# First layer's down projection as seven products, with the next mixer's input split beside its last steps

## The chip, the cores and the metric

The kernel runs on one core of one Trainium2 chip. The metric is the device time of one execution in microseconds (us), taken as the median of several runs; before the change it is 2800.11 us (three runs, 2799.79 to 2801.98).

## The reference, cut to what matters

One inference step of a two-layer encoder trunk on 1024 prompt frames and 32 sample frames (T = 1056 columns here), model width 1024:

```python
for i in range(DEPTH):                       # layer 0: retention, layer 1: GLA
    h = rmsnorm(x, norm_mix[i])
    x = x + mixer(h)
    h = rmsnorm(x, norm_ffn[i])
    u = h @ w_up                             # 1024 -> 2 * 2816
    c = causal_conv3(u) + conv_b
    gate, val = split(c)
    x = x + (silu(gate) * val) @ w_down      # 2816 -> 1024
y = rmsnorm(x, norm_final)
```

The change is about the last product of layer 0, `(silu(gate) * val) @ w_down`, and about the norm and first projections of layer 1's mixer (GLA) behind it. Everything is float32; each operand of a product is split into a rounded high part and a low remainder, and a product is three matmuls on TensorE: high by high, high by low, low by high.

## The kernel before, in words

**Layout.** The width lies on the partitions in tiles of 128, time lies along the free dimension. `XA`, `XB` and `XH` are large tiles that hold split operands; `AR` and `HR` hold float32 intermediates. `scr_x` in HBM holds the residual stream x. `R` holds the norm's factor for each column, the same on all partitions.

**Up projection** (`seven`, L331 to L441; `ffn_up`, L1905 on). It runs in both layers by seven products in place of eight: operands are cut into 2 by 2 quarters, sums of quarters are formed on VectorE, and a bank of 264 columns is accumulated for each of seven products (matmuls of lines 436, 440 and 441). After each of the 22 feature tiles `conv` makes the hidden tile. In layer 1 `pair_sums` (L1953 on) then forms the sums that seven products need and writes them to `scr_h7`; in layer 0 `conv` writes the plain hidden tile to `scr_h`.

**Down projection, layer 0** (`Down`, L1417 on). Three chunks of 384, 384 and 288 columns (`CM`); in each, 22 hidden tiles times 8 output tiles times 3 matmuls, lines 1519 to 1521. When a chunk is done, `evict` (L2221 on) adds the product to x (L2223), splits x for the mixer (`split_x`: ACT cast at L162, VectorE remainder at L163), squares it (`sumsq`, L147, and adds at L158 on VectorE and GpSimd in turn) and stores it. The norm of chunks 0 and 1 (`rms_a`, `rms_b`: L181 to L207) is made within the next chunk's steps, that of chunk 2 as a "tail" in the mixer's first steps. `rms_a` reduces the sum of squares over the partitions by matmuls against ones (L189), takes the root on ACT and VectorE (L174 to L179), and spreads it into a diagonal (`dg`, L199); `rms_b` multiplies the diagonal by ones (L205) and copies the result to `R` (L207).

**Down projection, layer 1** (`Down7`, L1602 on). Hidden tiles go in 11 pairs, output tiles in 4 pairs, and 14 windows n = 0 to 13 slide over the pairs: the widths are 1, 2, 3, eight times 4, 3, 2, 1 pairs. The windows of three and four take seven products, the others eight plain ones ("plain"), each over two column halves s, lines 1702 to 1704, 264 columns each. Up to window 9 the results are added to `scr_x` by accumulating DMAs on GpSimd's queue (L1769); from window 10 on they are added on VectorE to a fetched copy of x (`settle`, L1776 on, and L1719), squared (`squares`, L1796 on) and, behind the final norm (`row`, `root`, `out`), written as y. Weights come raw on SyncE's queue (L1649, L1654) and are split by ACT and VectorE (L1664, L1665; sums at L1684 to L1691).

**The mixer** (`gla`, L1050 on). Its first steps, in the order in which they are written: the gate's features for chunk 0 (`gates_in`, L1354 on; its result is scaled by `R` at L1361), the q and k products of head 0, chunk 0 (`proj`, L133 to L135), their scaling by `R` (`qk_out`), the gate (ACT and VectorE, with a scan at L1099), the tail norm of chunk 2, the features of chunks 1 and 2, then `weigh` (differences on GpSimd at L1122, exponentials on ACT, products on VectorE at L1128 and L1129) and the scores on TensorE (L1165 on).

**What sets the order.** The code is written step by step; a scheduler then orders each engine's queue by that order and by what it expects to be ready, so neighbouring steps may change places. An engine executes its own queue in order and waits at the first instruction whose inputs are not there. Tiles in a reused place wait for the last use of the old tile.

Of the kernel before, what the change touches and what calls it, by code (L numbers as in the profile page):

```python
# [9 lines left out]
F32 = mybir.dt.float32  # L10
# [6 lines left out]
P = 128  # L17
# [33 lines left out]
def trunk_kernel(ctx: ExitStack, tc: tile.TileContext, io):  # L51
# [129 lines left out]
    def rms_a(ss, c, ps, again=False, after=None):  # L181
        i = uid()
        if again and c == 2:
            for s_ in ss:
                G.tensor_copy(s_[:, 288:384].rearrange("p (j t) -> p j t", j=3),
                              s_[:, 256:288].unsqueeze(1).to_broadcast([P, 3, TS]))
        for m in range(3):
            for s_ in ss:
                mm = PE.matmul(ps[:, m:m + 1], s_[:, m * P:m * P + P], ones[:, 0:1],  # L189
                               start=s_ is ss[0], stop=s_ is ss[-1])  # L190
                if after is not None:
                    order(mm, after)
# [10 lines left out]
    def rms_b(dg, c, ps, copy=True):  # L203
        c0, n = CM[c]
        mm = PE.matmul(ps[:, :n], ones, dg.rearrange("p m t -> p (m t)")[:, :n], start=True, stop=True)  # L205
        if copy:
            S.copy(R[:, c0:c0 + n], ps[:, :n])  # L207
        return mm
# [266 lines left out]
    def gla_constants(gp):  # L475
# [7 lines left out]
        nc.sync.dma_start(ba, io["ba"])  # L483
        nc.sync.dma_start(smask, io["smask"])
        nc.sync.dma_start(dmask, io["dmask"])
        nc.sync.dma_start(lmask, io["lmask"])
# [9 lines left out]
        V.tensor_tensor(w2s[64:96], w2r, w2s[0:32].bitcast(F32), op=ALU.subtract)  # L496

# [552 lines left out]
    def gla(closers):  # L1050
# [303 lines left out]
        def gates_in(c):  # L1354
            c0, n = CM[c]
            ps = pp.tile([P, 512], F32, tag="pj", name=f"pa{c0}", bufs=2)
            for kt in range(KT):
                PE.matmul(ps[:32, :n], wa[:, kt], xh[:, kt, c0:c0 + n], start=kt == 0, stop=False)
                PE.matmul(ps[:32, :n], wa[:, kt], xl[:, kt, c0:c0 + n], start=False, stop=kt == KT - 1)
            ar = g1.tile([32, GH * GDK], F32, tag="asr", name=f"asr{c0}")  # L1360
# [16 lines left out]
        gates_in(1)  # L1377
        gates_in(2)
# [25 lines left out]
    scr_h = io["scr_h"]  # L1404
# [197 lines left out]
    class Down7:  # L1602

        def __init__(self, sm, regions, AR, HR):
            self.sm, self.AR, self.HR = sm, AR, HR
# [8 lines left out]
            homes = [list(range(7)), list(range(8, 15)), list(range(16, 22)) + [15], list(range(22, 28)) + [7]]  # L1614
            self.place = {(k, m): homes[k % 4][i] for k in range(NP) for i, m in enumerate(ORD)}
            self.place.update({(0, 8): 7, (1, 8): 15, (NP - 2, 8): 22, (NP - 1, 8): 23})
# [4 lines left out]
            self.sq = [HR[:, 4 * TH + j * TH:5 * TH + j * TH] for j in range(3)]  # L1621
# [23 lines left out]
        def raw_weights(self, n):  # L1645
            h, o = len(self.win[n]) * P, self.offs[n]
            if self.plain[n]:
                r = raw_tile(f"dr{uid()}")[:, :4 * h]
                nc.sync.dma_start(r, io["w_down7"][o:o + 4 * h * P].rearrange("(p c) -> p c", p=P))  # L1649
                return r  # L1650
            rs = []
            for j in range(2):
                r = raw_tile(f"d{'gv'[j]}{uid()}")[:, :2 * h]
                nc.sync.dma_start(r, io["w_down7"][o + j * 2 * h * P:o + (j + 1) * 2 * h * P].rearrange("(p c) -> p c", p=P))  # L1654
# [140 lines left out]

        def squares(self, p, s, half):  # L1796
            t0, n = 2 * TH * s + TH * half, TH
            y = self.Y[p][:, :, t0:t0 + n]
            ss = self.SS[s][:, TH * half:TH * half + n]
            for j in range(2):  # L1800
# [6 lines left out]
                (V if p == 2 and s and half else G).tensor_tensor(ss, ss, sq, op=ALU.add)  # L1807
# [27 lines left out]
        def early(self, s, i):  # L1835
            x0 = {1: [(0, 0, 2)], 2: [(0, 2, 2)], 3: [(0, 4, 2)], 4: [(0, 6, 2)], 5: [(1, 0, 2)], 6: [(1, 2, 2)]}
            x1 = {4: [(1, 4, 2)], 5: [(1, 6, 2)]}
            for a in (x1 if s else x0).get(i, []):
# [567 lines left out]
```

## Time and profile before

| | us |
|---|---|
| median of three runs | 2800.11 |
| lowest, highest | 2799.79, 2801.98 |
| the profiled execution's own time | 2802.62 |
| its span from first to last instruction | 2800.8 |
| layer 0's down projection in it (1340.44 to 1598.74) | 258.30 |
| layer 1's down projection in it (2544.06 to 2787.64) | 243.58 |

The granted TensorE clock of that execution is 0.997 of full speed. The profile page gives busy time by engine, the span in 40 slices, the chain of work that ended last, and groups of instructions by source line; the views of the trace used below are the table by stretches of time ("windows": length, then busy time and instruction count of each engine, granted clock, share of DMA busy, GB/s), the groups by line and shape (count, busy time, mean ns of one, idle time before), the waits, and the timeline.

### The profile page before, as it was taken

How to read it: one execution, taken by the hardware profiler on the slowest of the kernel's cores; microseconds unless marked ns; L12 is line 12 of the kernel's file. 1: busy time of each engine (PE TensorE's matmuls, PEld its weight loads, DVE VectorE, ACT ScalarE, POOL GpSimd, SP SyncE). 2: the span in 40 equal slices, each digit the busy share in tenths (PEclk: the TensorE clock that was granted, in tenths of full speed). 3: DMA queues.
4: the chain of work that ended last, by engine and by line, in shares of the span. 5: the costliest groups of instructions: out<-in, count | busy, mean ns of one | idle time of the engine just before them, and what ended most of it. 6: DMA issues, size and time to landing. Idle time of an engine off the chain costs nothing.

```text
span 2800.8 us, 54530 instructions
## 1 busy us (share of the span) xinstructions
PE 2758.4 (98%) x21990; PEld 2669.3 (95%) x21990; DVE 1972.2 (70%) x3387; ACT 1357.2 (48%) x2481; POOL 370.9 (13%) x637
## 2 busy tenths in 40 slices
PE   9999999999999999999999999999999999999997
PEld 9999988888999999999999989999999999999997
DVE  6876666676557877777555577775479888888666
ACT  7444354444435444444444466663355444445445
POOL 0000000000112111111000032220132111112113
PEclk9999999999999999999999999999999999999999
DMA  6233455554875222222855501115532433329783
GB/s 239 87 115 104 140 150 148 149 146 117 281 251 183 84 77 85 69 85 76 270 183 171 179 30 53 53 46 200 185 124 95 147 128 108 100 89 300 199 227 106
DMA packets 239006, 390.71 MB, mean 139 GB/s; under 512 B 58848, under 2 KB 163424, under 8 KB 234400
## 3 DMA queue, kind: packets, MB, share of 16 engines
q1 hardware_dynamic: 225712, 339.14, 37.3%
q0 software_dynamic: 12496, 47.54, 6.4%
q8 instruction: 172, 2.82, 0.4%
q14 instruction: 82, 0.67, 0.1%
q10 hardware_dynamic: 544, 0.54, 0.1%
HBM read 270.08 MB, written 117.07 MB: 138 GB/s over the span
## 4 chain that ended last, share of the span: by engine, by line
PE 81%; DVE 8%; ACT 3%; POOL 3%; issue 2%; DMA 2%; SPq 0%; DVEq 0%; ACTq 0%; POOLq 0%
PE pu L441 13%; PE pu L436 13%; PE pu L440 13%; PE pd L1519 6%; PE pd L1521 6%; PE pd L1520 6%; PE psv L270 2%; PE psv L271 2%; PE psv L272 2%; PE pu L1702 2%; POOL x L1122 2%; PE pu L1703 2%; PE pu L1704 2%; PE pg L133 1%; PE pg L134 1%
## 5 line engine op out<-in xcount | busy, mean ns | idle before, releaser
L110 DVE TENSOR_TENSOR wlo<-raw,whi 128x1024 fp32r<-128x1024 f32 x131 | 163.4, 1251 | 127.3 <-ACT whi L110 119.4
L415 ACT COPY HR<-pu 128x264 f32<-128x264 f32 x264 | 98.8, 375 | 278.6 <-PE pu L441 272.6
L110 ACT CAST whi<-raw 128x1024 fp32r<-128x1024 f32 x131 | 136.9, 1049 | 174.3 <-PE pd L1520 109.4
L441 PE MATMUL pu<-XA,wgl 128*128 128x264 f32 x752 | 213.4, 284 | 0.0
L436 PE MATMUL pu<-XA,wgh 128*128 128x264 f32 x752 | 212.8, 283 | 0.1
L440 PE MATMUL pu<-XA,wgh 128*128 128x264 f32 x752 | 212.5, 283 | 0.0
L1942 DVE SCALAR_TENSOR_TENSOR AR<-AR,cw 128x1058 f32<-128x1058 f32 x88 | 115.9, 1319 | 72.0 <-ACT AR L1941 63.7
L1915 DVE TENSOR_TENSOR AR<-HR,pu 128x264 f32<-128x264 f32 (+2 forms) x440 | 144.5, 370 | 4.5 <-PE pu L441 4.4
L1520 PE MATMUL pd<-hl,whi 128*128 128x384 f32 (+1 forms) x440 | 142.1, 323 | 0.1
L1519 PE MATMUL pd<-hh,whi 128*128 128x384 f32 (+1 forms) x440 | 142.1, 323 | 0.0
L1521 PE MATMUL pd<-hh,wlo 128*128 128x384 f32 (+1 forms) x440 | 141.7, 322 | 0.0
L436 PEld LDWEIGHTS pu<-XA,wgh 128*128 128x128 f32 x752 | 141.2, 188 | 0.3 <-ACT wgh L372 0.3
L440 PEld LDWEIGHTS pu<-XA,wgh 128*128 128x128 f32 x752 | 141.2, 188 | 0.0
L441 PEld LDWEIGHTS pu<-XA,wgl 128*128 128x128 f32 x752 | 141.0, 188 | 0.0
L436 PE MATMUL pu<-XA,wsh 128*128 128x264 f32 x464 | 132.5, 286 | 1.5 <-DVE ARi L927 0.4
L441 PE MATMUL pu<-XA,wtl 128*128 128x264 f32 x464 | 131.9, 284 | 0.0
L441 PE MATMUL pu<-XA,wsl 128*128 128x264 f32 x464 | 131.8, 284 | 0.0
L436 PE MATMUL pu<-XA,wth 128*128 128x264 f32 x464 | 131.6, 284 | 0.0
L440 PE MATMUL pu<-XA,wsh 128*128 128x264 f32 x464 | 131.4, 283 | 0.0
L440 PE MATMUL pu<-XA,wth 128*128 128x264 f32 x464 | 131.1, 283 | 0.0
L373 DVE TENSOR_TENSOR wtl<-rv,wth 128x1024 fp32r<-128x1024 f32 x58 | 71.0, 1224 | 79.0 <-ACT wth L372 78.9
L1939 POOL COPY cst<-AR 128x2 f32<-128x2 f32 x88 | 51.6, 586 | 564.9 <-DVE AR L1915 564.9
(643 smaller groups left out, 10616.9 us busy)
## 6 DMA issues: line engine op xcount, KB each, us to landing
raw<-w_down SPq DMA_DIRECT2D x60, 512.0 KB, 3.6
rg<-w_up SPq DMA_DIRECT2D x44, 512.0 KB, 3.6
rv<-w_up SPq DMA_DIRECT2D x44, 512.0 KB, 3.5
scr_h<-AR SPq DMA_DIRECT2D x81, 264.0 KB, 2.6
raw<-w_ro SPq DMA_DIRECT2D x39, 512.0 KB, 5.4
XH<-scr_hr POOLq DMA_DIRECT2D x16, 1056.0 KB, 7.1
scr_x<-AR POOLq DMA_DIRECT2D x60, 264.0 KB, 6.5
scr_h<-AR SPq DMA_DIRECT2D x22, 512.0 KB, 2.6
```

What stands on the lines that cost most here:

```text
L110: ins = S.copy(hi, raw), V.tensor_tensor(lo, raw, hi.bitcast(F32), op=ALU.subtract)
L270: PE.matmul(ps, ah, hi, start=kt == 0, stop=False)
L373: split_end[0] = split_last[0] = V.tensor_tensor(l_, src, h.bitcast(F32), op=ALU.subtract)
L415: ins = S.copy(t, b)
L436: mm = PE.matmul(ps, wh[:, k], x[:, 0, kt], start=m in (1, 2, 4, 5) and kt == 0, stop=False, skip_group_check=True)
L440: PE.matmul(ps, wh[:, k], x[:, 1, kt], start=False, stop=False, skip_group_check=True)
L441: mm = PE.matmul(ps, wl[:, k], x[:, 0, kt], start=False, stop=kt == 3, skip_group_check=True)
L1519: PE.matmul(o, w[0][:, k], h[0][:, :n], start=i == 0, stop=False)
L1520: PE.matmul(o, w[0][:, k], h[1][:, :n], start=False, stop=False)
L1521: self.last_mm = PE.matmul(o, w[1][:, k], h[0][:, :n], start=False, stop=i == nk - 1)
L1915: last_put[0] = V.tensor_tensor(u[:, d:d + n], t[:, o:o + n], b[:, o:o + n], op=op)
L1942: V.scalar_tensor_tensor(cj, uj[:, 1:T + 3], cw[:, nt, 1:2], cj, op0=ALU.mult, op1=ALU.add)
```

## The change

Layer 0 now uses `Down7` as layer 1 does, and `Down` is left for the mixers' output products only. Its parts:

1. `conv` calls `pair_sums` in both layers; `scr_h` and the plain branch go. `w_down7` holds both layers' weights.
2. In layer 0 the last windows run both halves of one window before the next window (`seq`), and the end of layer 0 squares 528 columns at a time into `R` (`new_squares`), splits x for the mixer and stores it to `scr_x` (`new_x`), at the steps that `news` lists. The first two mixer weights are loaded after a step of window 12 (`preload`).
3. The norm leaves the down projection. `rms_a` reads one sum of squares, from `R`, with 3 matmuls for a chunk in place of 12. The mixer begins with the q and k products of chunk 0, and each chunk's norm stands around that chunk's gate features (`features_of`).
4. The mixer's small constants are prepared behind the down projection and not ahead of it, the two weights first, the four masks after them.
5. In both layers: other places for the pairs (`homes`), other order of the first loads (`early`), the splits of the first pairs begin three steps earlier. In layer 1: GpSimd's share of the squares in window 13's second half moves to VectorE, and one output product (`out` of quarter 3, first part of the second half) moves from GpSimd to VectorE.

```diff
-    def rms_a(ss, c, ps, again=False, after=None):
+    def rms_a(c, ps):
         i = uid()
...
+        ss = [R[:, t0:t0 + L] for _, t0, L in minors(c)]
+        if c == 2:
+            ss[2] = nps[0].tile([P, 384], F32, tag="sq", name=f"sr{i}", bufs=sqb[0])[:, :P]
+            G.tensor_copy(ss[2].rearrange("p (j t) -> p j t", j=4),
+                          R[:, TP:T].unsqueeze(1).to_broadcast([P, 4, TS]))
         for m in range(3):
...
+            PE.matmul(ps[:, m:m + 1], ss[m], ones[:, 0:1], start=True, stop=True)
```

```diff
-        def gates_in(c):
+        def features_of(c):
             c0, n = CM[c]
-            ps = pp.tile([P, 512], F32, tag="pj", name=f"pa{c0}", bufs=2)
+            ps = lv("pa")
+            dg = rms_a(c, pp.tile([P, GDV], F32, tag="v", name=f"pn{uid()}", bufs=2))
             for kt in range(KT):
                 PE.matmul(ps[:32, :n], wa[:, kt], xh[:, kt, c0:c0 + n], start=kt == 0, stop=False)
                 PE.matmul(ps[:32, :n], wa[:, kt], xl[:, kt, c0:c0 + n], start=False, stop=kt == KT - 1)
+            rms_b(dg, c, lv("pr"))
...
-        gates_in(0)
         p00 = qk_products(0, 0)
+        features_of(0)
         q00 = qk_out(0, p00)
+        features_of(1)
         b00 = gate(0, 0)
-        run_tails(lv)
+        features_of(2)
         for f in closers:
             f()
         g2 = es.enter_context(pool("g2", side="right"))
         units = [(h, c) for h in range(GH) for c in range(3)]
-        gates_in(1)
-        gates_in(2)
```

```diff
+        def new_squares(self, p, s):
+            t = slice(2 * TH * s, 2 * TH * s + 2 * TH)
+            for j in range(2):
+                y = self.Y[p][:, j, t]
+                if p == 3 and j == 0:
+                    S.activation(R[:, t], y, AF.Square)
+                    continue
+                sq = self.sq[self.nsq % 3]
+                self.nsq += 1
+                S.activation(sq, y, AF.Square)
+                (V if p == 2 else G).tensor_tensor(R[:, t], R[:, t], sq, op=ALU.add)
+
+        def new_x(self, p, s):
+            t0, n = 2 * TH * s, 2 * TH
+            y = self.Y[p][:, :, t0:t0 + n]
+            for j in range(2):
+                split_x(2, y[:, j], 2 * p + j, t0, n)
+            nc.sync.dma_start(scr_x[:, 2 * p:2 * p + 2, t0:t0 + n], y)
...
-                (V if p == 2 and s and half else G).tensor_tensor(ss, ss, sq, op=ALU.add)
+                (V if p == 2 and s else G).tensor_tensor(ss, ss, sq, op=ALU.add)
```

```diff
+            else:
+                seq += [(n, s, i) for n in range(NP, N) for s in range(2) for i in range(4 if self.plain[n] else 7)]
...
+            new = self.new_x
+            news = {(1, 0, 1): [(new, 3, 0)], (1, 0, 3): [(new, 0, 0)], (1, 1, 1): [(new, 3, 1)], (1, 1, 3): [(new, 0, 1), (new, 1, 0)],
+                    (2, 1, 1): [(new, 2, 0)], (2, 1, 3): [(new, 1, 1), (new, 2, 1)]}
             for n, s, i in seq:
                 self.product(n, s, i)
                 k = n + 1
                 end = self.ends[n, s, i]
+                if n >= NP and not self.l:
+                    for f, *a in news.get((n - NP, s, i), []):
+                        f(*a)
+                    if (n, s, i) == (NP + 1, 0, 2):
+                        preload(*self.nxt)
```

```diff
-        if last:
-            down = Down7(sm, [(XA, 16), (XB, 8), (XH, 4)], AR, HR)
-        else:
-            down = Down(NF, lambda k: io["w_down"][l, k], lambda k: scr_h[k], CM, scr_x, sm, range(6, 9), 3)
+        down = Down7(l, sm, [(XA, 16), (XB, 8), (XH, 4)], AR, HR, nxt)
...
+        down.run(go.last_conv)
+        ex.close()
         gc = ExitStack()
-        gla_constants(gc.enter_context(pool("gc")))
...
+        if not last:
+            gla_constants(gc.enter_context(pool("gc")))
```

More of the change, by code (lines that the diff above doesn't have):

```diff
@@ L201, in rms_a, with rms_b @@
         return dg
-    def rms_b(dg, c, ps, copy=True):
+    def rms_b(dg, c, ps):
         c0, n = CM[c]
[L205 to L208, printed above, removed]
+        PE.matmul(ps[:, :n], ones, dg.rearrange("p m t -> p (m t)")[:, :n], start=True, stop=True)
+        S.copy(R[:, c0:c0 + n], ps[:, :n])
     table, last_silu = [None], [None]
@@ L1401, in gla @@
         es.close()
-    scr_h = io["scr_h"]
     tails = []
```

143 lines of the change are left out of this document (47 added, 96 removed).

## The prediction, before the changed kernel had run

> **What bounds the kernel now.** I read the page's busy shares first, then the slices of TensorE and its clock, then the chain of work that ended last.
>
> ```profile
> PE 2758.4 (98%) x21990; PEld 2669.3 (95%) x21990; DVE 1972.2 (70%) x3387; ACT 1357.2 (48%) x2481; POOL 370.9 (13%) x637
> ...
> PE   9999999999999999999999999999999999999997
> ...
> PEclk9999999999999999999999999999999999999999
> ...
> PE 81%; DVE 8%; ACT 3%; POOL 3%; issue 2%; DMA 2%; SPq 0%; DVEq 0%; ACTq 0%; POOLq 0%
> ```
>
> TensorE is busy 98% of the span at full clock and carries 81% of the chain. So only fewer columns through TensorE, or less of its idle time, moves the end; and whatever delays it once moves the end by as much. The table by stretches says what layer 0's down projection costs, what the seven-product one of layer 1 costs, and what surrounds them.
>
> ```profile
> 1340.44:1598.74 258.30, 258.08 (x1613) 256.62 (x1611) 137.31 (x189) 114.01 (x177) 8.79 (x10) 1.00 0.62 202
> ...
> 2544.06:2787.64 243.58, 234.19 (x1892) 231.48 (x1890) 169.37 (x276) 128.38 (x240) 62.50 (x70) 1.00 0.73 198
> 2600.00:2680.00 80.00, 80.00 (x658) 80.00 (x658) 52.04 (x84) 37.30 (x67) 13.04 (x15) 1.00 0.82 212
> 1598.74:1627.05 28.31, 27.84 (x166) 24.38 (x164) 24.80 (x49) 17.47 (x49) 11.74 (x15) 1.00 0.16 54
> ```
>
> The stretch that goes is 258.30 us long with 258.08 us of TensorE in it: there is no wait to win there, only work. The stretch of the same code that comes in its place, in layer 1, is 243.58 us with 234.19 busy: some 9.4 us of it are waits. The last row is the mixer's opening, from the end of the down projection to the first scores: TensorE is busy for 27.84 of 28.31 us, but VectorE for 24.80 as well, so it has little left to give there.
>
> **Term 1, the down projection.** Before: 22 x 8 x 3 chunks x 3 = 1584 matmuls of 384, 384 and 288 columns, 557,568 columns. After: the windows' widths 1, 2, 3, eight times 4, 3, 2, 1 add up to 44; the 38 of the wide ones take 7 products x 2 halves x 3 matmuls, the 6 of the plain ones 8 x 2 x 3: 1596 + 288 = 1884 matmuls of 264, 497,376 columns, 10.8% fewer. The undisturbed row has 658 in 80 us, 0.1216 us each: 1884 x 0.1216 = 229.1 us. That is the lower bound; layer 1's 243.58 is the upper, since it is measured with all waits. Which of these belong to layer 0 too, the waits of TensorE in that stretch and a little behind it tell:
>
> ```profile
> PE pu L1702 <- DVE AR L1760: 4.4, 5, 1.7
> PE pn L1814 <- DVE HR L1807: 2.0, 1, 2.0
> PE pn L1814 <- POOL HR L1807: 1.6, 1, 1.6
> PE pu L1702 <- DVE AR L1780: 1.5, 2, 1.0
> PE pu L1702 <- ACT AR L1752: 1.3, 1, 1.3
> PE pu L1702 <- ACT HR L1752: 0.3, 1, 0.3
> PE pu L1702 <- ACT HR L1756: 0.2, 1, 0.2
> ```
>
> The 1.6 us wait and the three small matmuls of `pn` belong to the final norm, which layer 0 doesn't have: with the restart behind it 2.4 us off. Of the L1780 waits the longer one, 1.0, stands behind the output products on VectorE (L1832): 1.2 off with its restart. (The 2.0 us wait lies behind the stretch.) The rest stays: the start (L1752, L1756) and the wide windows (L1760). So I take 240.0, and the term is 240.0 - 258.3 = **-18.3 us**, bounds -14.7 and -29.2.
>
> The DMAs go with this term: `Down7` in layer 1 issues the same weights, pieces and accumulating adds, on the same two queues, and its 243.58 us contain them. The two norms in the old stretch (24 small matmuls at L189 and four at L205) leave with it.
>
> **Term 2, the up projection.** Layer 0 now makes the pair sums, and each has one VectorE instruction more and its DMA. Layer 1 does so already:
>
> ```profile
> 1000.00:1100.00 100.00, 100.00 (x826) 100.00 (x826) 76.60 (x114) 45.62 (x65) 13.81 (x35) 1.00 0.24 81
> ...
> 2200.00:2300.00 100.00, 100.00 (x826) 100.00 (x826) 86.69 (x133) 47.65 (x69) 13.54 (x34) 1.00 0.40 138
> ```
> ```profile
> 894.33 0.90 PE pn L231 x4
> ...
> 2097.11 0.91 PE pn L231 x4
> ```
>
> VectorE rises from 76.60 to 86.69 in 100 us, TensorE stays at 100.00 with 826 matmuls: the sums are hidden. From the last norm's matmuls to the first of the down projection it is 2544.06 - 2097.11 = 446.95 in layer 1 and 1340.44 - 894.33 = 446.11 in layer 0: **+0.8 us**, bounds 0 and 1.5. Without that cover some 11 pairs x 4 sums x 0.70 (the 528-column remainder below) = 31 us would stand on VectorE's own path.
>
> **Term 3, the mixer's opening.** Here the cost lies. The groups by shape give the prices:
>
> ```profile
> L163 DVE SCALAR_TENSOR_TENSOR XA<-AR,gcol,XA 128x384 fp32r<-128x384 f32 x16 | 11.0, 688 | 0.2
> ...
> L163 DVE SCALAR_TENSOR_TENSOR XA<-AR,gcol,XA 128x288 fp32r<-128x288 f32 x7 | 3.8, 588 | 0.0
> ...
> L1719 DVE TENSOR_TENSOR AR<-AR,pu 128x264 f32<-128x264 f32 x16 | 6.7, 426 | 5.8 <-PE pu L1704 5.8
> ...
> L1642 DVE TENSOR_TENSOR XA<-XA 128x528 fp32r<-128x528 f32 x33 | 23.2, 703 | 2.2 <-ACT XA L1639 2.2
> ...
> L158 POOL TENSOR_TENSOR ss<-ss,sq 128x384 f32<-128x384 f32 x6 | 6.9, 1152 | 184.7 <-ACT sq L147 184.7
> ...
> L110 DVE TENSOR_TENSOR wlo<-raw,whi 128x1024 fp32r<-128x1024 f32 x131 | 163.4, 1251 | 127.3 <-ACT whi L110 119.4 <-PE pu L440 7.3
> ```
>
> VectorE in windows 12 and 13: 16 remainders of 528 columns, each 0.84 by the slope from 288 (588) to 384 (688), 13.4; 16 bank adds of 0.43, 6.8; 4 square adds of 528 at 0.70, 2.8; two mixer weights, 2.5: 25.5 us, and 1.5 until the first bank is ready. TensorE has 144 matmuls, 17.5 us. So VectorE ends about 9.5 us behind it. The remainders that chunk 0 still needs (tiles 4 and 5) end 5.65 us sooner (four remainders 3.4, two adds 0.85, two square adds 1.4), 21.3 us from the start of window 12; TensorE wants them at 17.5 + 12 x 0.174 = 19.6 (the first two rows below: 16 matmuls of 384 in 2.78 us), so it waits 1.7 us. Before, the opening had one wait of 0.34 us, and the scores began at 1627.05:
>
> ```profile
> 1598.74 0.34 PE L1358 MATMUL pa<-XA,wa 128*32 128x384 f32 x1
> ...
> 1601.52 0.34 PE L133 MATMUL pj<-XA,whi 128*128 128x384 f32 x1
> ...
> 1606.25 0.44 PE L133 MATMUL pj<-XA,whi 128*128 128x384 f32 x1 [0.34 <-DVE asr L1361]
> ...
> 1627.05 0.43 PE L1165 MATMUL pa<-q,k 128*32 128x128 f32 x8
> ```
> ```profile
> 1612.18 0.16 DVE L196 TENSOR_SCALAR tm<-pn 128x3 f32<-128x3 f32 x1 [0.85 <-PE pn L189]
> ...
> 1613.62 0.96 DVE L1099 TENSOR_TENSOR_SCAN b<-smask,t 128x384 f32<-128x384 f32 x1
> ...
> 1614.87 1.11 DVE L199 TENSOR_TENSOR dg<-ident,rc 128x384 f32<-128x384 f32 x1
> ...
> 1624.81 0.35 DVE L1129 TENSOR_TENSOR x<-x,q 128x192 f32<-128x192 f32 x1
> ```
>
> Then the norm: chunk 0 needs it before the features can be scaled, and TensorE's queue holds the matmul of `rms_b` with the next chunk's features, the gate and head 0's next q and k behind it. One such chain, 1612.18 to 1615.98 for the tail norm, takes 3.8 us with the gate mixed in; features of a chunk cover 16 x 0.174 = 2.8 of it. Counted from the end of the down projection: VectorE free at 9.5; R of chunk 0 at 13.3, its features and q at 16; second norm at 18; gate matmul 18.5; its ACT and VectorE steps end with the scan at 21.7. Before, the scan ended at 1614.58, 15.8 after the end, and the last product of `weigh` 10.2 us after that (1624.81), 2 us ahead of the scores, which began 28.3 after the end. With the scan at 21.7 they come at 31.9, 3.6 late; the third norm, and GpSimd's differences running against VectorE, add something: **+5 us**. Bounds: 0, if the scheduler fills every gap with other matmuls, and +21, the second rival below. I stand nearer to the low end, since the count above goes by measured rows.
>
> The constants' move puts two casts and two remainders behind the last product, where their place comes free, and six loads on SyncE's queue behind the x stores. The 48 q and k matmuls, 8.4 us, hide them. A weight that is eight times as large lands in 3.7 us, so without that cover it is some 5 us with the casts.
>
> ```profile
> raw<-w_gqk SPq DMA_DIRECT2D x8, 512.0 KB, 3.7
> ```
>
>  The norms' small matmuls here are 9 in place of 12, which I count as nothing.
>
> **Term 4, layer 1.** Earlier first splits can take at most the start's 1.8 us of L1752 and L1756 waits. At the end two square adds leave GpSimd (the 1.6 us wait), one output product of about 1 us joins VectorE's last three, which stand before the last norm's steps:
>
> ```profile
> 2789.65 3.05 DVE L1832 TENSOR_TENSOR AR<-AR,R 128x528 f32<-128x528 f32 x3
> ```
>
> **0 us**, bounds -3 and +1.5.
>
> **Sum:** -18.3 + 0.8 + 5 + 0 = -12.5 us against the profiled execution's own 2802.62, its span 2800.8 with 1.8 around it. The median, 2800.11, is 2.5 below; I take the difference from it: **2787.6 us**.
>
> **The rivals.**
>
> *The opening is free* (0.16). For it: the old opening shows TensorE filled across the tail norm. Against it: VectorE's 24.80 of 28.31 us. Term 3 is 0, and part of the start's waits goes in both layers: -12.5 - 5 - 2.5, about 2780.
>
> *GpSimd's square adds hold VectorE up* (0.14). Ten adds of 528 columns run on GpSimd in windows 10 to 12, 1.15 x 528/384 = 1.6 us each, 16 us, just where VectorE makes remainders from two SBUF operands. If each add stops VectorE for its whole length, VectorE ends 25 us behind TensorE, the opening costs 5 + 16 = 21 us, and the sum is +3.5: 2803.6, slower. It outweighs the gain from 17.5 us on, that is with 12.5 us of blocking. For it: `dg` (L199) took 1.11 beside GpSimd and 0.56 elsewhere.
>
> ```profile
> L199 DVE TENSOR_TENSOR dg<-ident,rc x3: 559/559/1108, 1445.6 to 1614.9; 128x384 f32<-128x384 f32 x3
> ```
>
> Against it: much of the 16 us falls where VectorE waits for banks anyway. (The Trainium skill, "SBUF — State Buffer", section "SBUF: two separate sides", calls the port pair of VectorE and GpSimd "an exclusive lock, not a bandwidth split", taken by VectorE operations with two SBUF inputs too. The doubled `dg` agrees; by that rule taken whole, the sum would be this rival's.)
>
> *Weights late in every window* (0.08). VectorE stands still until a window's raw weights have landed, with the bank adds queued behind:
>
> ```profile
> L1684 DVE TENSOR_TENSOR dv<-dv 128x512 f32<-128x512 f32 x8 | 5.5, 691 | 28.3 <-DMA dv<-w_down 28.3
> ...
> 2680.40 0.69 DVE L1684 TENSOR_TENSOR dv<-dv 128x512 f32<-128x512 f32 x1 [7.04 <-DMA dv<-w_down]
> ```
>
> In layer 1 this wait is 3.5 us on average and TensorE feels it only at 7: about 5.5 are absorbed. At 9.5 in each of eight windows TensorE would lose 4 x 8 = 32, of which 4.4 are counted: about 2815. It decides from a mean of 7.5 on. Against it: the same code, two windows in eight.
>
> That the change doesn't do what it says isn't open: the matmul count follows from the code.
>
> **How the numbers follow.** The forecast's own case, an opening of +2 to +9, gives 2784 to 2792, chance 0.62. About 0.2%, 5.6 us, is what a measurement of this kernel can tell from no change. Faster by more: 0.62 + 0.16 + 0.04 of the lock's case = 0.82; within: 0.07 of the lock's and 0.02 of the weights' = 0.09; slower: 0.03 + 0.06 = 0.09. The range 2777 to 2799 leaves out the weights' case, the lock's upper half and the tip of the free one: 0.18.
>
> **What would show it.** Right: 1884 matmuls at L1702's successors in layer 0 within 237 to 243 us; an up projection of 446 to 448; a first scores matmul some 33 us after the last product; a short TensorE wait on a remainder of tiles 4 or 5, and on `dg`. Wrong: a stretch above 246 with waits on L1684's weights; VectorE instructions of windows 11 to 13 at twice their length; scores at 28 or at 45; a change in the two stretches' surroundings that no term names.

## The result, and the profile after

The changed kernel takes 2798.47 us (median of 12 runs, 2796.24 to 2804.16) against 2800.24 us (12 runs) of the kernel before, measured side by side: ratio 0.9993, 95% interval 0.9985 to 1.0002. That can't be told from no change; the forecast was 12.5 us less. Run once more in another session (`e8_after_again`), it gave 2799.73 against 2801.81, 0.9993 again (0.9982 to 1.0004).

The page of the profile after, its busy shares and the slices of TensorE and its clock:

```profile
PE 2742.0 (98%) x22272; PEld 2652.5 (95%) x22272; DVE 2049.2 (73%) x3558; ACT 1369.6 (49%) x2520; POOL 403.6 (14%) x672
...
PE   9999999999999999999999999999999999999997
...
PEclk9999999999999999999999999999999999999999
```

TensorE is 16.4 us less busy than before and the span, 2795.6, is only 5.2 us shorter: some 11 us of the saved work came back as idle time. A slice is 70 us long, so nothing of this shows in the slices. The table by stretches of the same profile does show it (length, then busy time and count of TensorE, its weight loads, VectorE, ACT, GpSimd; then granted clock, DMA share, GB/s):

```profile
1340.26:1581.01 240.75, 233.57 (x1886) 231.70 (x1884) 172.09 (x269) 116.96 (x199) 50.57 (x51) 0.99 0.77 213
1581.01:1619.72 38.71, 31.82 (x174) 27.20 (x173) 30.62 (x66) 21.68 (x56) 10.31 (x12) 0.93 0.26 83
2535.11:2782.91 247.80, 238.13 (x1892) 235.84 (x1890) 168.04 (x275) 126.31 (x238) 59.56 (x67) 0.98 0.72 195
```

| stretch of the profiled execution | before | after | change | forecast |
|---|---|---|---|---|
| start to layer 0's down projection | 1340.44 | 1340.26 | -0.2 | +0.8 (term 2) |
| layer 0's down projection | 258.30 | 240.75 | -17.6 | -18.3 (term 1) |
| its end to the first scores | 28.31 | 38.71 | +10.4 | +5 (term 3) |
| first scores to layer 1's down projection | 917.01 | 915.39 | -1.6 | none |
| layer 1's down projection | 243.58 | 247.80 | +4.2 | 0 (term 4) |
| the rest | 13.16 | 12.69 | -0.5 | 0 (term 4) |

The column of changes sums to -5.2. From there to the -1.8 of the medians it is chance: the profiled execution of before lay 2.4 us above its median, the one of after 1.1 us below its own.

So the gain is there, and two stretches give it back. In layer 1's, TensorE has the same 1892 matmuls as before and is busy for 238.13 us instead of 234.19: the idle time in it is nearly the same (9.7 and 9.4 us), but the matmuls took 3.9 us longer, and the granted clock is 0.98 instead of 1.00. The waits of TensorE in the profile after, over the whole execution (total, times, longest):

```profile
PE pu L1695 <- DVE AR L1753: 8.9, 7, 2.6
PE pj L1081 <- DVE q L1071: 3.8, 1, 3.8
...
PE pj L133 <- ACT XA L162: 2.3, 2, 1.8
PE pu L1695 <- ACT XB L1632: 1.8, 2, 1.0
PE pu L1696 <- DVE XB L1635: 1.8, 2, 0.9
```

(Line 1695 is the former 1702, 1753 the former 1760, 1677 the former 1684.) And the stretches around five places where TensorE waited, in the table by stretches:

```profile
1358.00:1366.00 8.00, 6.12 (x36) 5.71 (x35) 6.33 (x7) 7.42 (x13) 2.62 (x3) 0.79 1.08 340
...
1616.00:1625.00 9.00, 5.87 (x171) 5.42 (x172) 7.14 (x18) 4.40 (x13) 1.03 (x2) 0.62 0.01 2
2553.00:2560.00 7.00, 5.24 (x28) 4.83 (x27) 5.60 (x6) 6.99 (x13) 2.62 (x3) 0.76 1.06 342
2571.00:2577.00 6.00, 3.69 (x18) 3.68 (x18) 5.65 (x9) 0.00 (x0) 2.64 (x3) 0.72 0.51 106
2719.00:2724.00 5.00, 3.84 (x19) 3.84 (x20) 4.63 (x9) 0.00 (x0) 1.06 (x2) 0.66 0.29 83
```

(The first and the third of these rows lie behind two waits of 0.9 us close together.) Behind each the clock is down: 0.72 over 6 us is 3.4 us at half speed, and so 1.7 us lost a second time. In the kernel before, layer 1's stretch had five L1760 waits, none over 1.71 us, and its clock stayed at 1.00.

### The profile page after: what moved, and what is told of

It is laid out like the page before. It is cut to its first block, busy times and chain, and to the rows that moved or that the text cites. A ratio compares the mean times of both kernels' runs of the same rounds, so it can differ in the third digit from the quotient of the medians.

```text
span 2795.6 us, 55418 instructions
## 1 busy us (share of the span) xinstructions
PE 2742.0 (98%) x22272; PEld 2652.5 (95%) x22272; DVE 2049.2 (73%) x3558; ACT 1369.6 (49%) x2520; POOL 403.6 (14%) x672
## 5 line engine op out<-in xcount | busy, mean ns | idle before, releaser
L1969 DVE SCALAR_TENSOR_TENSOR AR<-AR,cw 128x1058 f32<-128x1058 f32 x88 | 115.9, 1319 | 70.1 <-ACT AR L1968 62.9
L1512 PE MATMUL pd<-XH,whi 128*128 128x264 f32 x432 | 123.6, 286 | 0.0
L1514 PE MATMUL pd<-XH,wlo 128*128 128x264 f32 x432 | 122.3, 284 | 0.0
L1513 PE MATMUL pd<-XH,whi 128*128 128x264 f32 x432 | 122.2, 283 | 0.0
L1968 ACT ACTIVATE AR<-AR,cw 128x1058 f32<-128x1058 f32 x88 | 111.8, 1272 | 17.9 <-DVE AR L1942 16.4
L1970 DVE SCALAR_TENSOR_TENSOR AR<-AR,cw 128x1058 f32<-128x1058 f32 x88 | 115.7, 1316 | 0.0
L110 DVE TENSOR_TENSOR wlo<-raw,whi 128x1024 fp32r<-128x1024 f32 x74 | 94.9, 1289 | 26.7 <-ACT whi L110 21.7
```

The lines of the kernel that those rows point to most:

```text
L110: ins = S.copy(hi, raw), V.tensor_tensor(lo, raw, hi.bitcast(F32), op=ALU.subtract)
L1512: PE.matmul(o, w[0][:, k], h[0][:, :n], start=i == 0, stop=False)
L1513: PE.matmul(o, w[0][:, k], h[1][:, :n], start=False, stop=False)
L1514: self.last_mm = PE.matmul(o, w[1][:, k], h[0][:, :n], start=False, stop=i == nk - 1)
L1968: S.activation(cj, uj[:, 2:T + 4], AF.Identity, scale=cw[:, nt, 2:3], bias=cw[:, nt, 3:4])
L1969: V.scalar_tensor_tensor(cj, uj[:, 1:T + 3], cw[:, nt, 1:2], cj, op0=ALU.mult, op1=ALU.add)
```

## The experiments

**What VectorE stands before in the windows.** VectorE's timeline of the profile after, at the 2.31 us wait that TensorE has at 2573:

```profile
2568.07 0.42 DVE L1753 TENSOR_TENSOR AR<-AR,pu 128x264 f32<-128x264 f32 x1
2568.41 0.70 DVE L1635 TENSOR_TENSOR XB<-XB 128x528 fp32r<-128x528 f32 x1
2571.10 0.69 DVE L1677 TENSOR_TENSOR dv<-dv 128x512 f32<-128x512 f32 x1 [1.99 <-DMA dv<-w_down]
2571.71 1.22 DVE L1658 TENSOR_TENSOR dwtl<-dv,dwth 128x1024 fp32r<-128x1024 f32 x1
2572.84 0.42 DVE L1753 TENSOR_TENSOR AR<-AR,pu 128x264 f32<-128x264 f32 x1
```

The bank add of the first column half (L1753) is done at 2568.5; that of the second stands behind the next window's raw weights (L1677), which land only at 2571.1. TensorE needs the bank.

**e10** orders L1677 behind the second bank add (`self.seven` is that instruction) and prepares the next window's weights after the sixth product instead of the third (the two aren't tested apart):

```diff
-            V.tensor_tensor(rv[:, a], rv[:, a], rv[:, b], op=ALU.add)
+            ins = V.tensor_tensor(rv[:, a], rv[:, a], rv[:, b], op=ALU.add)
+            if behind is not None:
+                order(ins, behind)
...
-                    if 1 < k < NP and i == (2 if n > 1 else 1):
-                        self.weights(k, raws.pop(k))
+                    if 1 < k < NP and i == (5 if n > 1 else 1):
+                        self.weights(k, raws.pop(k), self.seven if n > 1 else None)
```

> In each wide window VectorE's first instruction on the next window's second raw weights (the sum in dv, L1677) is ordered behind the bank add of the second half (L1753), and the next weights are prepared after the sixth product. So VectorE no longer stands before weights that have not landed while a bank waits. Theory (these waits of 1.5 to 4 us at 1377, 1521, 2573 and 2720 us, each with 1.7 us of half clock, are what both layers' stretches lose): L1753 waits fall below 0.5 us, the two stretches lose 3 to 5 us each, 2790 to 2793. Rival (the raw tiles come free later, so each next window's weights are loaded later, and TensorE waits for the prepared weights instead): waits on dwsh and dwth appear, and the time is the same or up to 15 us longer.

It took 2789.7 us: 0.9959 of before (0.9947 to 0.9972), some 9 us less than the changed kernel and just under its theory's 2790 to 2793; by the rows below nearly all of it lies in layer 1 (9.1 us, layer 0 1.1). The two stretches in its profile, and the waits:

```profile
1341.68:1581.32 239.64, 232.82 (x1886) 231.41 (x1884) 173.40 (x270) 115.36 (x199) 50.62 (x52) 0.99 0.80 215
2535.80:2774.48 238.68, 232.94 (x1892) 231.23 (x1890) 168.48 (x275) 124.48 (x238) 60.62 (x67) 1.00 0.75 201
```
```profile
PE pu L1697 <- ACT AR L1751: 5.6, 2, 3.3
PE pj L1081 <- DVE q L1071: 3.8, 1, 3.8
```

The bank waits are gone, and layer 1's clock is back at 1.00 in this profile. (Averaged over the timed executions the granted clock is 0.994, as in the changed kernel, so over all of them the 9 us aren't the clock's.) A new wait of the same make has come up, on ACT: its cast of the summed weights stood 10.24 us before the DMA, with a block copy behind it for which TensorE waited.

```profile
1514.05 0.62 ACT L1683 CAST dwv<-dv 128x512 fp32r<-128x512 f32 x1 [10.24 <-DMA dv<-w_down]
1514.58 0.37 ACT L1751 COPY AR<-pu 128x264 f32<-128x264 f32 x1
```

**e13, e16 and e17: is it the change's, and what is left?** e13 puts the ordering of e10 on the kernel before. e16 has e10's ordering, the value weights of e2 (below), and ACT's cast ordered behind its copy of the seventh product's second half (`behind[0]`); e17 has both weight orderings on the kernel before. Edit of e16 and e17:

```diff
-            S.copy(v[:, a], rv[:, b])
+            ins = S.copy(v[:, a], rv[:, b])
+            if behind is not None:
+                order(ins, behind[0])
```

> The kernel before with the same ordering of the raw weights behind the banks in its layer 1. Theory A (these waits came with the change, its new order and its second stretch of seven products; before had 3 us of them in layer 1 and no half clock): 2797 to 2799.5, and the change is then worth 8 to 9 us. Theory B (layer 1 always paid them): layer 1's stretch falls from 243.6 to 239, the time to about 2796, and the change is then worth 6 us.

> As the kernel with both orderings (raw weights behind the banks on VectorE, value weights behind the x split), and ACT's cast of dwv ordered behind its block copy of the seventh product as well. Theory (that cast, which waits for weights with a block copy behind it, is what is left): TensorE's waits of 3.3 and 2.3 to 3.6 us behind L1753's copies go, with the half clock behind them, and the time falls by 5 to 8 us, to 2781 to 2784. Rival (the prepared weights then come too late, or the accumulating DMAs are what the copies wait for): 2787 to 2791, with TensorE waiting for dwv, dwsh or dwth instead.

> The kernel before with both orderings, VectorE's and ACT's, in its layer 1. Theory (its waits of 2.0 and 3.1 us behind block copies were the same cast standing before late weights): layer 1's stretch falls from 244 to 239 or 240 and the time to about 2796, so the change is worth 12 to 15 us once these waits are gone in both. Rival (those copies waited for the accumulating DMAs): 2799 to 2801.

e13: 2800.49, ratio 1.0000 (0.9991 to 1.0009): nothing gained, so theory B falls; theory A's small gain isn't seen either. Its profile has two block-copy waits of 2.0 and 3.1 us instead, each with a fall of the clock. e16: 2779.31, ratio 0.9916 (0.9902 to 0.9929), the shortest time here, 23 us under before and 2 us under its theory's range; its granted clock averages 0.997, as before's does. e17: 2797.58, 0.9984 (0.9975 to 0.9993), layer 1's stretch 240.0 us, as its theory said, though one block-copy wait of 2.3 us stays. The stretches of e16:

```profile
1341.48:1576.80 235.32, 230.70 (x1882) 229.51 (x1881) 172.16 (x270) 113.58 (x197) 50.92 (x52) 1.00 0.80 217
2531.25:2768.47 237.22, 232.80 (x1892) 231.14 (x1890) 168.04 (x275) 124.37 (x238) 60.33 (x67) 1.00 0.76 203
```

Counted to the same point as in the profile after (the row ends 0.5 us short of it), layer 0 takes 235.9 us at clock 1.00: 4.9 less. With both orderings the kernel before gains 0.16% and the changed one 0.77%; so these waits cost the changed kernel about 17 us more than the kernel before. (1.4 us of that may be the value weights', see e12.)

**Layer 1's part of the change, taken alone both ways.** e1 puts the old places, early loads, splits, squares and output order back in layer 1 of the changed kernel; e9 puts the new ones into layer 1 of the kernel before (its edit, in part; e1's is the reverse):

```diff
-            homes = [list(range(7)), list(range(8, 15)), list(range(16, 22)) + [15], list(range(22, 28)) + [7]]
+            homes = [[0, 1, 6, 7, 8, 9, 13], [2, 3, 4, 5, 10, 11, 12], list(range(16, 23)), [24, 25, 26, 27, 14, 15, 23]]
...
-                    if n == 0 and i < 2:
-                        self.first[6 + i](end)
+                    if n == 0 and self.first:
+                        self.first.pop(0)(end)
```

> Layer 1's down projection alone goes back to the places, early loads, split steps and output order of before; layer 0's stays as in the changed kernel. Theory (layer 1's start pays for the new order: an XB cast now stands behind a block copy that waits for an accumulating DMA): layer 1's stretch goes from 247.8 back to about 243.6 us, the first 314 matmuls from 46.05 to 42 us, the whole to about 2794.5 us. Rival (the 4.2 us are chance of one profiled execution, or come from where the weights lie after layer 0's change): the stretch stays above 246.5 and the time within 1 us of the changed kernel's 2798.5.

> The kernel before, with only layer 1's part of the change: the new places, early loads, split steps and output order. Layer 0 keeps its three products and the mixer its old opening. Theory (the new order costs 4.2 us in layer 1): the last stretch goes from 243.58 to about 247.5 us, the whole to about 2804.5. Rival (it costs nothing by itself): the stretch stays within 1.5 us of 243.6 and the time within 1.5 us of the kernel before.

e9: 2804.99 against 2801.81, ratio 1.0014 (1.0005 to 1.0022), layer 1's stretch 247.47 us. e1: 2797.47 against 2800.64, 0.9986 (0.9977 to 0.9995), stretch 242.68. Over all profiles that keep the schedule of before or after there, the old order took 242.4 to 243.6 us (three executions), the new one 243.9 to 249.5 (eight). So the new order costs some 4 us of the stretch. By the whole time it is 3.9 us in e9, clear of noise, but only 2 in e1, whose interval overlaps the changed kernel's (e1's theory had said 4). It costs them by the same mechanism; VectorE's timeline of e9 at its longest wait, where TensorE stands for 4.36 us:

```profile
2576.37 0.43 DVE L1760 TENSOR_TENSOR AR<-AR,pu 128x264 f32<-128x264 f32 x1
2576.71 0.71 DVE L1642 TENSOR_TENSOR XB<-XB 128x528 fp32r<-128x528 f32 x1
2580.48 0.69 DVE L1684 TENSOR_TENSOR dv<-dv 128x512 f32<-128x512 f32 x1 [3.06 <-DMA dv<-w_down]
2581.09 1.22 DVE L1665 TENSOR_TENSOR dwtl<-dv,dwth 128x1024 fp32r<-128x1024 f32 x1
2582.22 0.42 DVE L1760 TENSOR_TENSOR AR<-AR,pu 128x264 f32<-128x264 f32 x1
```

In the kernel before, the same raw weights stood behind both bank adds of that window. With the new order the scheduler filled VectorE's queue anew, and this instruction came out ahead; which of the moved steps did it isn't shown.

**e4** asks for the first splits of x pair 2 one product earlier in both layers, to take the start's waits on XB away: `(1, 1): (2, 0), (1, 2): (2, 1), (1, 3): (2, 2)` become `(1, 0)`, `(1, 1)`, `(1, 2)`.

> The first three splits of x pair 2 are asked for one product earlier, in both layers. Theory (the start's two waits of 0.9 us on XB, L1632 and L1635, which lie next to each other and are in some executions followed by the half clock, come from the place of those splits in the queues): the waits go in both layers, layer 0's stretch falls from about 242.9 to 240, layer 1's from 246.7 to 244, the whole by 4 to 6 us to about 2794. Rival (ACT stands before a block copy that waits for an accumulating DMA, so the casts can't run sooner wherever they are asked for): both stretches stay within 1 us of these and the time within 1 us of the changed kernel's 2798.5 to 2799.7.

2806.22, ratio 1.0021 (1.0011 to 1.0031): neither theory. The XB waits went, and others of 0.5 to 0.8 us on block copies took their place; the raw weights stand ahead of the second bank add once more, and the waits behind them at 1380 and 2581 are now 6.3 and 5.4 us in its profile:

```profile
PE pu L1695 <- DVE AR L1753: 17.8, 9, 6.3
```

**GpSimd's additions.** e3 and e14 leave GpSimd's additions out, e3 in the changed kernel, e14 in e10, so the norm's sum lacks those tiles; e15 moves them to VectorE in e10. The edit of e3:

```diff
-                (V if p == 2 else G).tensor_tensor(R[:, t], R[:, t], sq, op=ALU.add)
+                if p == 2:
+                    V.tensor_tensor(R[:, t], R[:, t], sq, op=ALU.add)
```

> Leaves out the additions of squares that GpSimd makes in layer 0's last windows (the mixer's norm then lacks those tiles in its sum); VectorE's four additions stay. Theory in which GpSimd's additions hold VectorE up: the remainders L163 beside them fall from 1.3 to 2.5 us each to about 0.8, VectorE is free 5 to 6 us sooner, and the stretch from the last product to the first scores goes from 38.7 to 33 to 35 us, the whole to about 2793.5. Rival (VectorE waits for banks and x there anyway, so the stretching is absorbed): the opening changes by less than 1.5 us.

> The ordering of the raw weights, and GpSimd's additions of squares in layer 0 left out (the mixer's norm lacks those tiles in its sum). Theory (they hold VectorE up by 6.4 us, and 4 to 5 us of that reach the opening): opening from 39.2 to 34 or 35 us, the whole 4 to 5.5 us below 2789.7, 2784 to 2786. Rival (the earlier kernel without them was faster through fewer weights' waits and not through the opening): within 2 us of 2789.7.

> The ordering of the raw weights, and all the additions of squares in layer 0 on VectorE: ten more of about 0.70 us each there, none on GpSimd. Theory (VectorE loses 6.4 us beside GpSimd's additions in the last 60 us, and some of the ten fall where it has time): the remainders take 0.77 us each again, opening 37.5 to 39.5 us, the whole from 2788 to 2790.5. Rival (VectorE's queue is the bound and seven more us in it outweigh what it was held up): opening 40 us and more, 2791 to 2793.

e3: 2790.57, 0.9969 (0.9957 to 0.9981). e14: 2782.64, 0.9938 (0.9924 to 0.9951), some 6 us under e10 by the ratios. VectorE's groups by shape from 1540 to 1600 us, first of the profile after, then of e3:

```profile
L163 DVE SCALAR_TENSOR_TENSOR XA<-AR,gcol,XA 128x528 fp32r<-128x528 f32 x16 | 15.2, 971 | 1.1 <-ACT XA L162 1.1
L110 DVE TENSOR_TENSOR wlo<-raw,whi 128x1024 fp32r<-128x1024 f32 x4 | 8.0, 1991 | 0.0
```
```profile
L163 DVE SCALAR_TENSOR_TENSOR XA<-AR,gcol,XA 128x528 fp32r<-128x528 f32 x16 | 11.9, 766 | 0.0
L110 DVE TENSOR_TENSOR wlo<-raw,whi 128x1024 fp32r<-128x1024 f32 x4 | 4.9, 1219 | 0.0
```

The same sixteen remainders take 3.3 us less and the four weight remainders 3.1 us less. The opening falls from 38.71 us to 33.3 in e3, and in e14 to 33.4 from e10's 39.8 (row of e14; it begins 0.45 us ahead of the point from which 38.71 is counted, and the openings here and below are counted from that point):

```profile
1575.30:1609.17 33.87, 30.04 (x179) 26.16 (x177) 26.02 (x58) 19.35 (x53) 8.98 (x11) 0.97 0.27 88
```

That is the forecast's 33 us. How the remainders reach the end is seen on TensorE, first in the profile after, then in e3:

```profile
1585.80 0.44 PE L133 MATMUL pj<-XA,whi 128*128 128x384 f32 x1 [1.83 <-ACT XA L162]
1587.03 0.69 PE L134 MATMUL pj<-XA,whi 128*128 128x384 f32 x1 [0.78 <-DVE XA L163]
1594.74 0.72 PE L189 MATMUL pn<-ones,R 128*128 128x1 f32 x6
```
```profile
1590.09 0.72 PE L189 MATMUL pn<-ones,R 128*128 128x1 f32 x6
```

The q and k products wait 3.1 us for the split of x (0.45 of it ahead of these rows), and the clock is at half for 3.4 us from 1586.9 on. So the norm's small matmuls, which stand behind them in TensorE's queue, begin 13.7 us after the last product. In e3 nothing of this waits, and they begin after 8.4.

In e15 (2790.32, 0.9959, 0.9947 to 0.9972) the remainders also take 765 ns, but VectorE has 7 us more to do, and the opening is 38.8 us: a draw, as expected.

**The value weights.** In the profile after, two remainders of the mixer's value weights (L110 at 1573.37 and 1581.40, 2.34 and 2.13 us) stand between the x remainders. e2 orders them behind the last one (`x_done` is the last cast and the last remainder of the split); e11 adds that to e1, e12 adds it to e10.

```diff
-                wv[h] = [load_w(io["w_gv"][h, t], None, (None, second_mask[0])) for t in range(2)]
+                wv[h] = [load_w(io["w_gv"][h, t], None, (None, second_mask[0]) if h else x_done) for t in range(2)]
```

> The mixer's first value weights (cast and remainder of w_gv for head 0) are ordered behind the last remainder of the x split; nothing else changes. Theory (VectorE's backlog at the opening was made longer by them, 2.34 and 2.13 us ahead of the splits): VectorE ends the splits at about +7.5 us instead of +12.1 after the last product, TensorE's waits on XA shrink, and the stretch from the last product to the first scores goes from 38.7 to 34 or 35 us; the whole to about 2794.5. Rival (the norm chains in series set the opening, not the backlog): the stretch stays at 37.5 to 39.

> Both single steps that made their stretch shorter, together: layer 1's places, loads and order as before, and the first value weights behind the x split. Theory (they lie in different stretches, so they add up): opening 36.2 us, layer 1's stretch 243, the whole 4 to 5 us under the changed kernel, about 2794.5. Rival (differences of single profiled executions): within 1.5 us of the changed kernel.

> The ordering of the raw weights behind the banks, and the mixer's first value weights behind the x split, together. Theory (backlog on VectorE sets the opening, and the value weights are 2 to 2.5 us of it): opening 39.2 to 37, the whole 2 us under the 2789.7 of the first ordering alone, about 2787.5. Rival (nothing, as the whole showed when only the value weights were moved): 2789 to 2791.

2799.3 (0.9996, 0.9988 to 1.0005), 2796.43 (0.9983, 0.9974 to 0.9991) and 2789.1 (0.9954, 0.9942 to 0.9967). The opening is 36.2 us in e2 and 36.1 in e12, 2.5 less than in the profile after and 3.6 less than in e10, but in e2 the stretch behind it is 1.7 longer, and of the whole time nothing certain is left: 0.9959 and 0.9954 can't be told apart, and e11 lies between its theory's 4 to 5 us and none. In e16, which has the same ordering, the opening is 39.3 us again: its profile has 6.8 us at half clock from 1593.5 on, behind a wait of 1.28 us for `dg`, and e12's has none before the gate's wait.

**The norm's place, the gate's bank, and a filler.** e5 issues chunk 0's norm between the q and the k products. e6 gives the gate matmul of chunk 1, which waits 3.83 us for VectorE to empty its bank, a bank of the other ring. e7 puts twenty matmuls without use ahead of it.

```diff
-            pz = t384(pp, "pj", w=512)
+            pz = lv("pz") if (h, c) == (0, 1) else t384(pp, "pj", w=512)
```
```diff
+                pd = pp.tile([P, GDV], F32, tag="v", name=f"pd{uid()}", bufs=2)
...
+                for i in range(20):
+                    d = PE.matmul(pd, xh[:, 0, 0:P], xh[:, 1, 0:GDV], start=True, stop=True)
...
```

> The three small norm matmuls of chunk 0 (and the root and diagonal behind them) are issued between the q and the k products of head 0 rather than behind both. Theory (the norm chains in series are on the path): R of chunk 0 stands about 4 us sooner, the opening goes from 38.7 to about 35 us, the whole to about 2795. Rival (VectorE's backlog sets it, and the root then waits in VectorE's queue behind the remainders, or delays them): the opening stays within 1 us, or grows by up to 2, since the small matmuls now wait for the last squares in the middle of the q and k products.

> The gate matmul of chunk 1 writes to a bank of the other ring (lv) rather than waiting until VectorE has read the q product of chunk 1 from its own (pj); the order of the instructions on all engines is that of the changed kernel. Theory (TensorE's 3.83 us wait there, with the half clock that follows it in the profile, from 1617 to 1625 us, is on the path): the wait falls below 1 us, the granted clock stays at 1.00 over the first scores, and the stretch from the last product to the first scores goes from 38.1 to 34 or 35 us; the work behind it gains the half clock's 2.5 us only if the scores themselves are on the path. Whole: 2794 to 2796. Rival (what VectorE has in its queue sets the end of the first unit, and TensorE only waits elsewhere): the first scores come sooner, but the stretch from the last product to layer 1's norm stays within 1 us of the changed kernel's 484.6.

> Twenty matmuls of 256 columns, whose result nobody reads, stand ahead of the same gate matmul, 2.3 us of the 3.83 us in which TensorE waits there. Theory (a wait of 2 us and more is followed by some 3.4 us or more at half clock, and that is a second price of the wait): the clock stays at 1.00 from 1615 to 1626, the first scores begin where they did (38.1 us after the last product, within 0.5), and what lies behind them comes about 2.5 us sooner. Rival (the low clock doesn't come from the wait, or what runs in it isn't on the path): the clock falls in the same place, or the stretch from the last product to layer 1's norm stays at 484.6 within 1 us; matmuls that are of no use can't make it faster in any other way.

e5: 2801.68, 1.0003 (0.9994 to 1.0012); its opening is 37.65 us, about 1 less: the rival holds, the chain of the norm alone isn't what sets it. e6: 2798.9, 0.9991 (0.9982 to 1.0000). The first scores come 4 us sooner (34.28 us), and then TensorE waits nearly as long a little further on, for the next step of VectorE:

```profile
PE pl L1179 <- DVE t L1087: 3.5, 1, 3.5
```

From the last product to layer 1's norm it is 1.9 us less than in the profile after, of which e6's rival allowed 1. So VectorE's queue is most of what bounds this stretch, and the bank a small part; of the whole time nothing certain is left. e7: 2798.68, 0.9985 (0.9975 to 0.9994). The row of its profile, to be held against a clock of 0.66 in the same ten microseconds of the profile after:

```profile
1616.00:1626.00 10.00, 7.52 (x199) 6.76 (x198) 8.94 (x22) 5.62 (x19) 2.20 (x5) 1.00 0.01 2
```

The clock stays at 1.00, the scores begin where they did (38.68), and what follows, up to layer 1's norm, is 1.1 us shorter. So the half clock does come from the wait, but the 2.5 us that e7's theory expected of it aren't there. That the 1.1 us are the filler's can't be told from noise by the whole time (0.9985 and 0.9993 overlap).

> The changed kernel once more, in the same session as the others. Theory in which layer 1's 247.8 us is the new order's: again 246.5 to 249. Rival (weights and x that land sooner or later decide in each execution how many waits pass the point from which the clock falls): layer 1's stretch lies anywhere from 243 to 248, with one to three falls of the clock in it, each 1.7 us.

e8's stretch of layer 1 is 246.03 us with one fall of the clock, that of layer 0 243.61 with two. Its rival holds in so far as the stretches vary from execution to execution; that the new order is dearer on the average, e9 shows.

## Why the prediction was wrong, step by step

- **Term 1** was right in its mechanism and nearly in its size: 240.0 was said, 240.75 measured in the profile, 242.5 on average over six executions of kernels that leave this stretch alone (after, e1, e5 to e8; 240.8 to 243.8). "The rest stays" was where it failed. In the profile the one fall of the clock stands behind the start's two waits of 0.97 and 0.90 us; in seven others (e1 to e3, e5 to e8) one stands behind a wide window's wait of 2.1 to 3.7 us, longer than any that was kept.
- **Term 2** was right: from the last norm's matmuls, at 893.67 in the profile after, to the down projection it is 446.59 us, +0.5 (+0.8 said).
- **Term 3** had the right chain and the wrong size: +10.4 for +5. VectorE was done with the splits 12.1 us after the last product (9.5 said), `R` of chunk 0 stood at 18.4 (13.3), the scan ended at 26.1 (21.7). The sum priced the remainders at 0.84 us each; beside GpSimd they took 0.97, and the two mixer weights that it took at 1.25 each took 2.34 and 2.13 (they are the value weights; those of q and k came a window earlier). It let TensorE wait 1.7 us for the split and put nothing on the clock; TensorE waited 3.1 and ran 3.4 us at half clock. And it began the norm's chain, 3.8 us, when VectorE was free; the chain began only when TensorE had reached the small matmuls, 1.6 us later, and `R` stood 6.3 us after VectorE's last remainder. e3 gives 5.4 us back, e14 6.4 against e10. The rival that named this mechanism stood beside the sum with its full 16 us, and none of it was taken into the sum, though the quoted row of `dg` showed a doubling.
- **Term 4** was wrong: layer 1's stretch cost 4.2 us (e9: 3.9). The sum asked what each moved step costs and what it frees, but not what the scheduler would put ahead of what in VectorE's queue.
- **The third rival**, weights late in every window, went by the mean length of VectorE's wait before the weights. In the view of the tile `dv` that was 36.2 us in 7 waits in layer 1 before and 35.1 in 8 after, no more; what counts is whether a bank add or a block copy stands behind the waiting instruction. So the mechanism was the right one, and the point from which it was to decide, a mean of 7.5 us, was the wrong measure. e10 and e16 show what it was worth: 9 us and, with ACT's cast and the value weights, some 21 us.
- **Left out altogether** was the half clock. In layer 1 it is 3.9 of the 4.2 us. Averaged over the timed executions the granted clock is 0.997 before and 0.994 after; 0.0026 of 2800 us is up to 7 us of TensorE's work (an estimate from these two means).

In numbers, against the profiled pair: forecast -12.5; term 1 +0.75, term 2 with what stands ahead of it -1.0, term 3 +5.4, term 4 with the rest +3.7, the stretch without a term -1.6; together -5.2. Once the waits are ordered away (e10), the changed kernel stands at 2789.7, inside the 2784 to 2792 of the forecast's own case, but by luck of another sum: its opening is 39.8 us and not 33, and layer 1's stretch is 4.9 us shorter than before's.

What stays open: which of layer 1's moved steps put the raw weights ahead of the bank add, and how the 11 us that the opening still takes above before's with e16 (39.3 us in its profile) could be had without taking GpSimd's additions away.

## What to carry to other kernels

When a step is moved, read off which instructions that wait for a DMA end up ahead of which bank adds and copies in each in-order queue: the waiting itself is cheap until something that TensorE needs stands behind it. Add some 1.7 us to a TensorE wait of about 2 us and more, for the half clock that mostly follows it. A stretch taken over from elsewhere in the kernel brings its waits along, but their length belongs to the queues around it, not to the code.

## What the runs showed of the hardware

**The clock falls after short waits.** In the traces of before, after and e1 to e15 (every TensorE wait of 1.3 us or more in the two down projections and the opening up to 1630 us, the norm's own waits at the end left aside, each with the granted clock of the 4 us behind it): of 14 waits up to 1.71 us none was followed by a lower clock; of 38 between 1.75 and 3.3 us, 27 were; of 24 from 3.35 us on, all. Mostly 3.4 us then ran at half speed. The Trainium skill, "TensorE: Matmul & The Clock Gate", section "Part 1: The HAM clock gate (the "warmup" mystery)", has a free-running window of about 3.4 us and calls for at least one idle window; the 3.4 us at half speed agree, but half of such a wait is enough here.

What decides between 1.75 and 3.3 us is where the wait lies. In each of the 19 traces all falls of the clock start a whole number of 3.413 us from one another, to 0.01 us. Divided along this grid, from 20 to 2775 us, the share of a step at full clock in which TensorE is idle tells the clock of the next step: of 15,158 steps idle for less than 45%, one was followed by half clock; of 27 between 45 and 55%, 7; of 55 above, all. Half a step is 1.71 us, so a single wait below that can't fill half of one, a wait of 3.4 us fills half of some step wherever it lies, and two waits of 0.9 us can add up in one step.

**GpSimd's adds cost VectorE less than their length.** Ten additions of 528 columns, 14.3 us on GpSimd, took 7.3 us from VectorE: 3.3 on the remainders of x, 3.1 on four weight remainders of the mixer and 1.0 on one of window 12's (L1658, 2.19 us, in e3 1.22). A pair of remainders beside one took 2.52 us instead of 1.44, a weight remainder 2.28 instead of 1.22. The Trainium skill, "SBUF — State Buffer", section "SBUF: two separate sides", has an exclusive lock for each instruction; the single lengthened instructions agree, and the rest of the 14.3 us fell where VectorE waited or worked on banks.
